# Block products of a decoder layer: high and low weights in two runs, all of the up projection in the 512-column form, and the conv's taps by ScalarE and adding DMAs

## The chip, the cores and the metric

The kernel runs on one core of one Trainium2 chip. The metric is the time of one execution on the device in microseconds (us); lower is better. Before the change it is 2632.48 us, the median of 3 runs (2631.31 to 2634.93).

## What is computed

The reference is one decoder layer over 512 tokens of width 2048, in float32. Cut to what matters here:

```python
proj = x @ w_in                        # (512, 2048) @ (2048, 12288)
u, gate_b, gate_c, q, k, v = split(proj)
y_conv = gate_b * causal_conv3(gate_c * u, conv_w)
y_attn = dilated_window_attention(q, k, v)      # three patterns, merged
x = layernorm(ALPHA * x + concat(y_conv, y_attn) @ w_out)
up = causal_conv3(x @ w_up, ffn_conv_w) + ffn_conv_b   # (512, 2048) @ (2048, 11264)
a, g = split(up)
out = layernorm(ALPHA * x + (silu(g) * a) @ w_down)

def causal_conv3(x, w):                # along the tokens, zero before the first
    return w[0] * x[t-2] + w[1] * x[t-1] + w[2] * x[t]
```

The change touches the two projections `x @ w_in` and `x @ w_up`, and the conv behind the second.

## The kernel before

**High and low parts.** A float32 matrix is kept as two matrices in the format float32r, which TensorE multiplies: a rounded copy `hi` and the rest `lo = x - hi`. A product of two matrices is hi·hi + hi·lo + lo·hi. ScalarE makes `hi` of a weight block (L217), VectorE makes `lo` (L220); both are 128x1024, and both are made up to four blocks ahead of TensorE (the ring `RING = 4`, tiles `whi` and `wlo`).

**Pairs and products.** The projections are cut into pairs of two 128-column strips of the weights: 48 pairs for `w_in`, 44 for `w_up` (`FT`). A pair is computed by Winograd's form of Strassen's scheme: the weights of a pair are four blocks B11, B12, B21, B22, the activations four blocks A11 to A22, and seven products (numbered 1 to 7 in the table `PROD`) replace eight. Four of them take sums of weight blocks, T1 to T4, which VectorE makes with one 128x1024 subtraction each (L207), into tiles `tt` of their own. The products of a pair gather in four PSUM regions: x1 takes products 1, 6, 7; x2 takes 2; x3 takes 5, 3; x4 takes 4. ScalarE copies a region out ("snapshot") after product 1 (x1), 5 (x3) and 6 (x1), before the next product of that region adds to it. VectorE then adds regions and snapshots together (`combine`) into the pair's output tile `o`.

**Two forms of a product.** In the narrow form (`product`, L362 to L374) each of 8 weight slices takes three matmuls with 256 columns: hi·hi (L371), hi·lo (L372), lo·hi (L373), 24 in all. In the 512-column form (`product_wide`, L342 to L352) hi·hi and hi·lo are one matmul with 512 columns (L349), followed by one with 256 (L351), 16 in all; region x2 or another then fills a whole PSUM bank, its halves are still to be added, and `combine` (L418) has four parts with two VectorE instructions each (L427 and L1129 or L683/L687) where the narrow form has two with one each (L667). The part of x4 also takes a ScalarE copy of x1 (L424).

**Which pair takes which form.** Pair 0 of each projection is computed in plain products; of pairs 1 to 5 ("pre-pairs") products 1 and 2 are computed early, while the activations' sums are still being made, and the other five in the narrow form. In the input projection all 42 other pairs take the 512-column form. In the up projection `every=3` (L456, L1131) gives it to the 13 pairs from 6 on whose number divides by 3; the other 25 take the narrow form.

**What sets the order.** Nothing is scheduled by a planner: each engine runs its instructions as they are written. For each product the program writes the matmuls, the snapshot, then `free` (L254), which lets the next weight block be read (`front`, L202: T sum and `hi`) and the one before it be finished (`back`, L219: `lo`), and then `tick` (L321), which runs work that `later(n, ...)` put off by n products. A `combine` is put off by 2. The order of a pair's products is the list `MAIN = [1, 5, 6, 3, 7, 4, 2]` (`LAST` for the last pair); pre-pairs take it without 1 and 2. Weights come in by SP's queue into `RAWS = 3` tiles `raw` of 1 MB, and a tile is loaded again when all blocks in it have been used.

**Behind a pair of the up projection** (`done3`, L1107): ScalarE scales both strips by the conv's tap 2 and adds the bias (L1112); one product later VectorE adds taps 1 and 0 of the gate strip (`taps`, L691 to L694, two instructions) and ScalarE takes Silu (L1116); two products later VectorE adds the taps of the value strip, and three products later it multiplies both (L1119); a DMA from POOL's queue writes the result to DRAM (L1120). POOL's queue holds nothing else in this stage.

## Time and profile before

| | |
|---|---|
| median of 3 runs | 2632.48 us |
| profiled execution, its own time | 2634.48 us |
| its span, first to last instruction | 2632.7 us |
| granted TensorE clock, mean | 0.997 |
| TensorE (PE) busy | 2595.9 us, 99% |
| weight loads (PEld) busy | 2323.1 us, 88% |
| VectorE (DVE) busy | 2157.0 us, 82% |
| ScalarE (ACT) busy | 1211.6 us, 46% |
| GpSimd (POOL) busy | 125.7 us, 5% |

How to read it: the profile is one execution, 1.8 us of whose time lies outside the span. PE counts as busy while a matmul is in its pipeline, so neighbouring matmuls overlap in it, and the sum of a group's durations is more than what the group takes: for the pace one reads the starts in the timeline. In the timeline a row has start, duration, engine, line, operation, output<-inputs, shapes, count, and in brackets the idle time of the engine before it with what ended it. The input projection runs to about 974 us, the attention, the output projection and the first layer norm to about 1245 us, the up projection to 2140 us, the down projection to the end.

### The profile page before, as it was taken

What the parts mean: (1) busy time and instruction counts of PE and PEld (TensorE: products, weight loads), DVE (VectorE), ACT (ScalarE), POOL (GpSimd) and SP (SyncE); (2) the same over time, 40 slices, a digit from 0 to 9 for tenths busy, and PEclk for the clock granted to TensorE, in tenths of its full rate; (3) what the DMA queues carried; (4) which work ended last, traced back from release to release, by engine and by line L of the source; (5) the groups of instructions that cost most, each with busy time, mean ns of one, the idle gap of its engine ahead of it and who ended that gap; (6) DMA issues with size and microseconds to landing.
All of it is one profiled execution on the core that took longest, in us unless ns stands there. A gap on an engine that the chain in (4) does not pass through costs nothing.

```text
span 2632.7 us, 39148 instructions
## 1 busy us (share of the span) xinstructions
PE 2595.9 (99%) x16034; PEld 2323.1 (88%) x16034; DVE 2157.0 (82%) x2575; ACT 1211.6 (46%) x1617; POOL 125.7 (5%) x217
## 2 busy tenths in 40 slices
PE   9999999999999989999999999999999999999997
PEld 8988888888888878888999999999999988888886
DVE  7989888888888877657899999999998966765557
ACT  5544444444444444434655555555555553222220
POOL 0000100000000002220000000000000000000000
PEclk9999999999999999999999999999999999999999
DMA  7422543333333357653543333333333353434331
GB/s 243 169 102 108 182 148 129 132 138 132 128 140 133 125 208 257 220 184 105 184 148 125 118 119 112 121 122 116 123 118 119 125 204 140 152 124 160 112 128 64
DMA packets 70229, 376.34 MB, mean 143 GB/s; under 512 B 9921, under 2 KB 13793, under 8 KB 35361
## 3 DMA queue, kind: packets, MB, share of 16 engines
q1 hardware_dynamic: 51680, 311.47, 33.6%
q0 software_dynamic: 18368, 62.36, 6.5%
q8 instruction: 126, 2.06, 0.3%
q14 instruction: 55, 0.44, 0.1%
HBM read 328.61 MB, written 48.84 MB: 143 GB/s over the span
## 4 chain that ended last, share of the span: by engine, by line
PE 90%; DVE 5%; DMA 2%; ACT 2%; issue 1%; SPq 0%; POOL 0%; DVEq 0%; ACTq 0%
PE bk L349 27%; PE bk L351 13%; PE bk L514 8%; PE bk L516 8%; PE bk L515 8%; PE bk L371 8%; PE bk L372 8%; PE bk L373 8%; DVE wlo L220 1%; DVE tt L207 1%; DMA raw<-in_w_in_dram 1%; DMA ycr<-yc_d 1%; PE bk L848 1%; ACT whi L217 1%; PE bk L794 0%
## 5 line engine op out<-in xcount | busy, mean ns | idle before, releaser
L217 ACT ACTIVATE whi<-raw 128x1024 fp32r<-128x1024 f32 x394 | 414.5, 1057 | 586.5 <-PE bk L516 210.4
L349 PE MATMUL bk<-S,whi 128*128 128x512 f32 x1760 | 624.4, 399 | 1.4 <-ACT s L446 1.4
L220 DVE TENSOR_TENSOR wlo<-raw,whi 128x1024 fp32r<-128x1024 f32 x394 | 480.0, 1221 | 151.3 <-ACT whi L217 149.8
L217 ACT ACTIVATE whi<-tt 128x1024 fp32r<-128x1024 f32 x360 | 381.2, 1059 | 364.2 <-PE bk L349 157.4
L351 PE MATMUL bk<-S,wlo 128*128 128x256 f32 x1760 | 494.1, 281 | 0.0
L349 PE MATMUL bk<-A,whi 128*128 128x512 f32 x1320 | 469.9, 399 | 0.0
L220 DVE TENSOR_TENSOR wlo<-tt,whi 128x1024 fp32r<-128x1024 f32 x360 | 439.4, 1221 | 33.7 <-ACT whi L217 30.1
L349 PEld LDWEIGHTS bk<-S,whi 128*128 128x128 f32 x1760 | 330.7, 188 | 84.5 <-ACT s L446 2.1
L351 PE MATMUL bk<-A,wlo 128*128 128x256 f32 x1320 | 370.7, 281 | 0.0
L351 PEld LDWEIGHTS bk<-S,wlo 128*128 128x128 f32 x1760 | 332.4, 189 | 0.0
L371 PE MATMUL bk<-S,whi 128*128 128x256 f32 x1152 | 326.5, 283 | 1.8 <-ACT sm L467 0.9
L372 PE MATMUL bk<-S,whi 128*128 128x256 f32 x1152 | 326.0, 283 | 0.0
L373 PE MATMUL bk<-S,wlo 128*128 128x256 f32 x1152 | 326.0, 283 | 0.0
L349 PEld LDWEIGHTS bk<-A,whi 128*128 128x128 f32 x1320 | 248.1, 188 | 62.4 <-issue 1.5
L371 PE MATMUL bk<-A,whi 128*128 128x256 f32 x936 | 265.9, 284 | 2.2 <-ACT A L312 1.2
L373 PE MATMUL bk<-A,wlo 128*128 128x256 f32 x936 | 265.3, 283 | 2.6 <-DVE wlo L220 2.6
L372 PE MATMUL bk<-A,whi 128*128 128x256 f32 x936 | 265.0, 283 | 0.9 <-DVE A L313 0.9
L351 PEld LDWEIGHTS bk<-A,wlo 128*128 128x128 f32 x1320 | 249.4, 189 | 0.0
L371 PEld LDWEIGHTS bk<-S,whi 128*128 128x128 f32 x1152 | 221.1, 192 | 2.8 <-ACT z L467 1.7
L372 PEld LDWEIGHTS bk<-S,whi 128*128 128x128 f32 x1152 | 221.1, 192 | 0.0
L373 PEld LDWEIGHTS bk<-S,wlo 128*128 128x128 f32 x1152 | 221.1, 192 | 0.0
L207 DVE TENSOR_TENSOR tt<-raw,tt 128x1024 f32<-128x1024 f32 x180 | 219.1, 1217 | 0.0
(206 smaller groups left out, 4154.0 us busy)
## 6 DMA issues: line engine op xcount, KB each, us to landing
raw<-in_w_in_dram SPq DMA_DIRECT2D x97, 1024.0 KB, 4.9
raw<-in_w_up_dram SPq DMA_DIRECT2D x89, 1024.0 KB, 5.3
raw<-in_w_down_dram SPq DMA_DIRECT2D x44, 1024.0 KB, 4.9
qkv_d<-o POOLq DMA_DIRECT2D x36, 512.0 KB, 3.8
raw<-in_w_out_dram SPq DMA_DIRECT2D x16, 1024.0 KB, 7.3
act_d<-z POOLq DMA_DIRECT2D x44, 256.0 KB, 5.1
qk<-qkv_d SPq DMA_DIRECT2D x7, 1536.0 KB, 10.3
ar<-act_d SPq DMA_DIRECT2D x9, 1024.0 KB, 7.0
```

What stands on the lines that cost most here:

```text
L207: nc.vector.tensor_sub(self.src, v[0], prev)
L217: nc.scalar.activation(self.hi, self.src, AF.Copy)
L220: nc.vector.tensor_sub(self.lo, self.src, self.hi.bitcast(F32))
L349: mm(ps, op.hi[:, w], X[xn].both(k), start=first and k == 0, stop=False, skip_group_check=True)
L351: mm(ps[:, 256:], op.lo[:, w], X[xn][0][:, k], start=False, stop=last and k == 7, skip_group_check=True)
L371: mm(ps, op.hi[:, w], xh[:, k], start=first and k == 0, stop=False, skip_group_check=True)
L372: mm(ps, op.hi[:, w], xl[:, k], start=False, stop=False, skip_group_check=True)
L373: mm(ps, op.lo[:, w], xh[:, k], start=False, stop=last and k == 7, skip_group_check=True)
L514: mm(banks[n], yh[:, tt], op.hi[:, w], start=first and i == 0, stop=False)
L515: mm(banks[n], yh[:, tt], op.lo[:, w], start=False, stop=False)
L516: mm(banks[n], yl[:, tt], op.hi[:, w], start=False, stop=last and i == 1)
L848: nc.tensor.transpose(ps[:, i * P:(i + 1) * P], src[:, n, s:s + P], ident)
```

## The change

1. **High weights first.** In both forms of a product the 8 slices of `hi` run first, then the 8 slices of `lo`. Before, each slice's `lo` matmul followed its `hi`.
2. **All pairs of the up projection from 6 on take the 512-column form** (`every` goes).
3. **Weight sums in place.** T1 and T2 are written over B12, T3 over B11, T4 over B21, inside the `raw` tile; the `tt` tiles go, and `RAWS` is 4. What T2 overwrites must have been used, so the order of products changes: `MAIN` is `[1, 5, 2, 6, 3, 7, 4]` for all pairs, and the pre-pairs take `REST = [5, 3, 6, 7, 4]`. The sums of activations (`s_first`, `s_rest`) use tiles `o` as scratch.
4. **Conv taps of the up projection by ScalarE and DMAs.** For every pair but the last, `done3` has ScalarE multiply both strips by tap 1 into a tile `t` and by tap 0 in place, and two DMAs from POOL's queue add them, shifted by 1 and 2 tokens, to `cv` (`accum_op=OP.add`). Silu follows 7 products later (`TAPS`), the multiplication 8.
5. Tiles: `o` has 5 buffers in this stage, `z` has 4; `cv` is now a tile `o`.

```diff
-RAWS = 3
+RAWS = 4
+TAPS = 7
-MAIN = [1, 5, 6, 3, 7, 4, 2]
-LAST = [1, 5, 2, 6, 3, 7, 4]
+MAIN = [1, 5, 2, 6, 3, 7, 4]
+REST = [5, 3, 6, 7, 4]
...
             if self.kind[0] == "T":
-                self.src = tt_tile()
-                prev = v[1] if len(v) > 1 else self.box["T1" if self.kind == "T2" else "T2"]
-                nc.vector.tensor_sub(self.src, v[0], prev)
-                self.box[self.kind] = self.src
+                b = self.box
+                if self.kind == "T1":
+                    b["T"] = v[0]
+                    nc.vector.tensor_sub(b["T"], v[0], v[1])
+                elif self.kind == "T2":
+                    nc.vector.tensor_sub(b["T"], v[0], b["T"])
+                else:
+                    nc.vector.tensor_sub(v[0], v[0], b["T"])
+                self.src = b["T"] if self.kind in ("T1", "T2") else v[0]
...
-        parts = {"B11": [b11], "B21": [b21], "B22": [b22], "T1": [b12, b11], "T2": [b22], "T3": [b12, b22],
-                 "T4": [b21]}
+        parts = {"B11": [b11], "B21": [b21], "B22": [b22], "T1": [b12, b11], "T2": [b22, b12], "T3": [b11, b12],
+                 "T4": [b21, b12]}
...
-            mm(ps, op.hi[:, w], X[xn].both(k), start=first and k == 0, stop=False,
-               skip_group_check=True)
+            mm(ps, op.hi[:, w], X[xn].both(k), start=first and k == 0, stop=False, skip_group_check=True)
+        for k in range(8):
+            w = slice(k * P, (k + 1) * P)
             mm(ps[:, 256:], op.lo[:, w], X[xn][0][:, k], start=False, stop=last and k == 7, skip_group_check=True)
...
     def done3(j, o):
         o = o.rearrange("p (f h) t -> p f (h t)", f=2)
-        cv = [stile3() for _ in range(2)]
+        cv = otile3().rearrange("p (f h) t -> p f (h t)", f=2)
         for f in range(2):
             ft = j + f * FT
-            nc.scalar.activation(cv[f], o[:, f], AF.Identity, bias=fw_t[:, ft, 3:4], scale=fw_t[:, ft, 2:3])
+            nc.scalar.activation(cv[:, f], o[:, f], AF.Identity, bias=fw_t[:, ft, 3:4], scale=fw_t[:, ft, 2:3])
+        if j < FT - 1:
+            for sh in (1, 2):
+                t = otile3().rearrange("p (f h) t -> p f (h t)", f=2) if sh == 1 else o
+                for f in range(2):
+                    ft = j + f * FT
+                    nc.scalar.activation(t[:, f], o[:, f], AF.Copy, scale=fw_t[:, ft, 2 - sh:3 - sh])
+                nc.gpsimd.dma_start(cv[:, :, sh:], t[:, :, :S - sh], accum_op=OP.add)
...
-        later(1, gate)
-        later(2, lambda: taps(cv[0], o[:, 0], fw_t[:, j]))
-        later(3, mul)
+        later(1 if j == FT - 1 else TAPS, gate)
+        later(2 if j == FT - 1 else TAPS + 1, mul)
...
-    run_pairs(plan3, X, stile3, otile3, bands, done3, act_first, block3, 3)
+    run_pairs(plan3, X, stile3, otile3, bands, done3, act_first, block3)
```

Three places in the order of the instructions. First, on PE, product 6 of a pair in the input projection (S are the chunks of the activation sum S2, `whi` and `wlo` the weight block's two parts, `bk` the PSUM bank), the first six of eight slices of it before (of each two slices that read alike, one):

```order
L349 MATMUL bk_203_1608<-S_66_440,whi_1574 128x512
L351 MATMUL bk_203_1608<-S_66_440,wlo_1575 128x256
...
L349 MATMUL bk_203_1608<-S_76_514,whi_1574 128x512
L351 MATMUL bk_203_1608<-S_76_514,wlo_1575 128x256
...
L349 MATMUL bk_203_1608<-S_85_585,whi_1574 128x512
L351 MATMUL bk_203_1608<-S_85_585,wlo_1575 128x256
```

and the whole of such a product now:

```order
L353 MATMUL bk_206_1756<-S_67_442,whi_1750 128x512 x2
L353 MATMUL bk_206_1756<-S_77_516,whi_1750 128x512 x2
L353 MATMUL bk_206_1756<-S_86_587,whi_1750 128x512 x2
L353 MATMUL bk_206_1756<-S_93_662,whi_1750 128x512 x2
L356 MATMUL bk_206_1756<-S_67_442,wlo_1751 128x256 x2
L356 MATMUL bk_206_1756<-S_77_516,wlo_1751 128x256 x2
L356 MATMUL bk_206_1756<-S_86_587,wlo_1751 128x256 x2
L356 MATMUL bk_206_1756<-S_93_662,wlo_1751 128x256 x2
```

The alternation of 512 and 256 columns has become a run of eight of each, and `wlo` is first read eight matmuls later.

Second, on ACT, the stretch behind a finished pair of the up projection in the 512-column form. Before (L446 are the snapshots of products 1, 5 and 6 into `z`, L217 makes `whi`, L1112 is the conv's tap 2, L1116 is Silu):

```order
L217 ACTIVATE whi_18000<-raw_17847 128x1024
L446 ACTIVATE z_18023<-bk_2680_18006 128x512
L217 ACTIVATE whi_18027<-tt_18025 128x1024
L1112 ACTIVATE z_18032<-o_18004,fw_t 128x512
L1112 ACTIVATE z_18033<-o_18004,fw_t 128x512
L446 ACTIVATE z_18053<-bk_2687_18036 128x512
L217 ACTIVATE whi_18057<-tt_18055 128x1024
L1116 ACTIVATE z_18033<-z_18033 128x512
L446 ACTIVATE z_18082<-bk_2680_18006 128x512
L217 ACTIVATE whi_18084<-raw_17847 128x1024
```

and now (L453 are the snapshots, L221 makes `whi`, L1133 is Silu of the pair before, L431 the copy of x1, L1121 tap 2 into `cv`, L1127 taps 1 and 0):

```order
L221 ACTIVATE whi_15736<-raw_15486 128x1024
L453 ACTIVATE z_15759<-bk_2247_15742 128x512
L221 ACTIVATE whi_15761<-raw_15488 128x1024
L1133 ACTIVATE o_15588<-o_15588 128x512
L431 ACTIVATE z_15766<-bk_2220_15560 128x512
L1121 ACTIVATE o_15770<-o_15672,fw_t 128x512 x2
L1127 ACTIVATE o_15773<-o_15672,fw_t 128x512 x2
L1127 ACTIVATE o_15672<-o_15672,fw_t 128x512 x2
L453 ACTIVATE z_15797<-bk_2254_15780 128x512
L221 ACTIVATE whi_15800<-raw_15486 128x1024
L221 ACTIVATE whi_15824<-raw_15488 128x1024
L453 ACTIVATE z_15844<-bk_2247_15742 128x512
```

Between the snapshot of product 1 and that of product 5 stood three instructions (a weight block and two tap copies); now there are nine.

Third, on ACT, the second pre-pair of the input projection. Before (`sm` takes the snapshots of products 1 and 5, `sn` those of 6 and 7; the blocks `whi` are those of the end of this pair and the start of the next; L705 belongs to the mixer's conv):

```order
L467 ACTIVATE sm_946<-bk_34_182 128x256
L467 ACTIVATE sm_946<-bk_126_949 128x256
L217 ACTIVATE whi_977<-tt_975 128x1024
L705 ACTIVATE o_817<-o_944,cw_t 128x512 x2
L467 ACTIVATE sn_947<-bk_34_182 128x256
L217 ACTIVATE whi_1014<-tt_1012 128x1024
L217 ACTIVATE whi_1048<-tt_1046 128x1024
L467 ACTIVATE sn_947<-bk_34_182 128x256
L217 ACTIVATE whi_1079<-raw_981 128x1024
```

and now:

```order
L474 ACTIVATE sm_941<-bk_35_184 128x256
L474 ACTIVATE sm_941<-bk_120_944 128x256
L221 ACTIVATE whi_971<-raw_654 128x1024
L711 ACTIVATE o_813<-o_939,cw_t 128x512 x2
L221 ACTIVATE whi_1004<-raw_847 128x1024
L474 ACTIVATE sn_942<-bk_35_184 128x256
L221 ACTIVATE whi_1039<-raw_849 128x1024
L474 ACTIVATE sn_942<-bk_35_184 128x256
L221 ACTIVATE whi_1071<-raw_847 128x1024
```

The snapshot of product 6 (the first `sn`) stands one product later, and that of product 7 follows it after one block instead of two: product 7, which adds to the same region, now follows product 6 at once, and product 3 follows product 5, with whose region it shares x3.

More of the change, by code (lines that the diff above doesn't have):

```diff
@@ L183, in load_next @@
         st["load"] += 1
-    def tt_tile():
-        return wpool.tile([P, UNIT], F32, tag="tt", name=nm("tt"), bufs=3)
     class Op:
@@ L290, in plan @@
         for p in range(nplain, n):
-            seqs.append((p, [q for q in (LAST if p == n - 1 else MAIN) if p >= nplain + npre or q > 2], False))
+            seqs.append((p, MAIN if p >= nplain + npre else REST, False))
         return seqs
@@ L372, in product @@
                 mm(ps, op.hi[:, w], xl[:, k], start=False, stop=False, skip_group_check=True)
+            for k in range(8):
+                w = slice(k * P, (k + 1) * P)
                 mm(ps, op.lo[:, w], xh[:, k], start=False, stop=last and k == 7, skip_group_check=True)
@@ L454, in run_wide, with run_pairs @@
                 hook(p, q)
-    def run_pairs(pl, X, stile, otile, bands, done, hook=None, put_block=None, every=1):
+    def run_pairs(pl, X, stile, otile, bands, done, hook=None, put_block=None):
         for p, seq, pre in pl:
@@ L459, in run_pairs @@
                 continue
-            if 1 in seq and put_block and p % every == 0:
+            if 1 in seq and put_block:
                 run_wide(p, seq, X, stile, otile, put_block, done, hook)
@@ L579, in layer_kernel, with otile1 @@
     tp = mkpool(tps, "tp1", "right")
+    def otile1():
+        return tp.tile([P, 4, 256], F32, tag="o", name=nm("o"), bufs=3)
     def x_load(i, k):
@@ L586, in x_split @@
         split(X[n][0][:, k:k + 2], X[n][1][:, k:k + 2], raw["S2"][k // 2][:, i])
-    wt = tt_tile()[:, :256 + P]
+    wt = otile1().rearrange("p a t -> p (a t)")[:, :256 + P]
     nc.vector.memset(wt, 0.0)
@@ L621, in layer_kernel @@
         plan_work(XS + i // 2, x_split, 1, 2 * i)
-        plan_work(XF[i], s_first, X, raw, 2 * i)
-        plan_work(XR[i], s_rest, X, raw, 2 * i)
+        plan_work(XF[i], s_first, X, raw, 2 * i, otile1)
+        plan_work(XR[i], s_rest, X, raw, 2 * i, otile1)
     hook = schedule(todo)
@@ L636, in layer_kernel @@
     nc.sync.dma_start(gb_t, lnc)
-    def otile1():
-        return tp.tile([P, 4, 256], F32, tag="o", name=nm("o"), bufs=3)
     def bias_setup(g=0):
@@ L945, in otile3 @@
     def otile3():
-        return chp.tile([P, 4, 256], F32, tag="o", name=nm("o"), bufs=2)
+        return chp.tile([P, 4, 256], F32, tag="o", name=nm("o"), bufs=5)
     def keep3():
@@ L951, in stile3, with ztiles @@
     def stile3(b=None):
-        return zbp.tile([P, 512], F32, tag="z", name=nm("z"), bufs=8)
-    def ztile(t):
-        return stile3() if t >= 2 else zap.tile([P, 512], F32, tag="z", name=nm("z"), bufs=8)
-    z = [[ztile(t) for c in range(4)] for t in range(4)]
+        return zbp.tile([P, 512], F32, tag="z", name=nm("z"), bufs=4)
+    def ztiles(t):
+        if t == 2:
+            return [o.rearrange("p (a b) t -> p a (b t)", a=2)[:, i] for o in (otile3(), otile3()) for i in range(2)]
+        return [stile3() if t == 3 else zap.tile([P, 512], F32, tag="z", name=nm("z"), bufs=8) for c in range(4)]
+    z = [ztiles(t) for t in range(4)]
     for c in range(4):
@@ L1073, in layer_kernel @@
         plan_work(HF + 2 * i + 1, tr_k, 2 * i + 1, 1, raw["S4"])
-        plan_work(HF + 2 * i + 1, s_first, X, raw, 2 * i)
-        plan_work(HR[i], s_rest, X, raw, 2 * i)
+        plan_work(HF + 2 * i + 1, s_first, X, raw, 2 * i, otile3)
+        plan_work(HR[i], s_rest, X, raw, 2 * i, otile3)
     hook = schedule(todo)
```

20 lines of the change are left out of this document (11 added, 9 removed).

## The prediction

> **What bounds the kernel now.** I read the page first, then the busy time by stretches, then PE's timeline in each stage, since the pace of the matmuls is all that can change the time of a stage in which PE never waits.
>
> ```profile
> span 2632.7 us, 39148 instructions
> PE 2595.9 (99%) x16034; PEld 2323.1 (88%) x16034; DVE 2157.0 (82%) x2575; ACT 1211.6 (46%) x1617; POOL 125.7 (5%) x217
> PE 90%; DVE 5%; DMA 2%; ACT 2%; issue 1%; SPq 0%; POOL 0%; DVEq 0%; ACTq 0%
> ```
>
> PE is busy for 99% of the span and carries 90% of the chain that ended last (third row). So the kernel is bound by TensorE, and an edit pays where it shortens TensorE's own work. How near the others are shows in two stretches of 200 and 100 us, one in each projection (PE, PEld, DVE, ACT, POOL busy, clock, DMA share, GB/s):
>
> ```profile
> 400.00:600.00 200.00, 200.00 (x1135) 173.42 (x1134) 174.88 (x192) 96.77 (x112) 7.16 (x10) 1.00 0.37 132
> 1700.00:1800.00 100.00, 100.00 (x782) 97.32 (x781) 91.46 (x100) 53.57 (x72) 2.71 (x5) 1.00 0.35 119
> ```
>
> VectorE stands at 87% in the input projection and at 91% in the up projection. The paces come from the starts of matmuls in PE's timeline: the 512-column form, then the narrow form, then, from the down projection, 512-column matmuls that follow one another.
>
> ```profile
> 599.61 0.40 PE L349 MATMUL bk<-A,whi 128*128 128x512 f32 x1
> ...
> 627.88 0.40 PE L349 MATMUL bk<-S,whi 128*128 128x512 f32 x1
> ```
>
> ```profile
> 1470.05 0.28 PE L371 MATMUL bk<-S,whi 128*128 128x256 f32 x1
> ...
> 1475.81 0.28 PE L371 MATMUL bk<-A,whi 128*128 128x256 f32 x1
> ```
>
> ```profile
> 2249.72 0.39 PE L514 MATMUL bk<-whi,ah 128*128 128x512 f32 x1
> ...
> 2255.84 0.39 PE L514 MATMUL bk<-whi,ah 128*128 128x512 f32 x1
> ```
>
> Between the first two rows lie 80 slices (ten products): 28.27 us, 0.353 for a 512 and a 256, 2.827 a product. Between the second two lie 48 matmuls (two products): 5.76 us, 0.120 each, 2.88 a product. Between the last two lie 27: 6.12 us, 0.227 each. So the two forms differ by only 0.05 us a product, and a 512 and a 256, each among its like, would take 0.227 + 0.120 = 0.347 where the alternation takes 0.353.
>
> ```profile
> L349 PE MATMUL bk<-A,whi x312: 395/398/403, 1379.0 to 2119.7; 128*128 128x512 f32 x156
> L371 PE MATMUL bk<-A,whi x603: 281/283/283, 1377.9 to 2139.9; 128*128 128x256 f32 x151
> ```
>
> Pairs 6 to 43 of the up projection run from 1379.0 to about 2140 (both rows, with the last slices): 761 us, 20.03 a pair. The 13 wide pairs (91 products at 2.827) and 25 narrow (175 at 2.88) make 257 + 504 = 761: PE does not wait there at all.
>
> **The change, part by part.**
>
> *High weights first.* A product becomes eight 512s and eight 256s: 8 x 0.347, plus about 0.01 for the two changes of width, 2.78 us against 2.827. The input projection has 42 such pairs, 294 products: 294 x 0.047 = **-13.8 us**. VectorE's 87% becomes 89% of the shorter time. [...]
>
> *All pairs wide.* Pairs 6 to 43 now take 266 x 2.78 = 739.5 us if PE still never waits: **-21.8 us**. What covers that is VectorE and ScalarE.
>
> ```profile
> 1701.02 0.69 DVE L427 TENSOR_TENSOR z<-bk,z 128x512 f32<-128x512 f32 x1 [1.61 <-ACT z L424]
> 1701.75 0.43 DVE L1129 TENSOR_TENSOR o<-z 128x256 f32<-128x256 f32 x1
> 1702.09 1.22 DVE L207 TENSOR_TENSOR tt<-raw,raw 128x1024 f32<-128x1024 f32 x1
> 1703.23 1.22 DVE L220 TENSOR_TENSOR wlo<-raw,whi 128x1024 fp32r<-128x1024 f32 x1
> L693 DVE SCALAR_TENSOR_TENSOR z<-o,fw_t,z 128x510 f32<-128x510 f32 x88 | 66.0, 750 | 3.1
> L1119 DVE TENSOR_TENSOR z<-z,z 128x512 f32<-128x512 f32 x44 | 30.1, 684 | 0.1
> ```
>
> From start to start VectorE pays 0.73 for a region's addition, 0.34 for the half's, 1.14 for a 128x1024 subtraction. A pair has 7 `lo`, 4 sums, 4 + 4 additions and the multiplication (684 ns, less the overlap, 0.6): 11 x 1.14 + 4 x 1.07 + 0.6 = 17.4 us of 19.5. Without the taps it fits; with them (four of 750 ns, less the overlap, 2.7 us) it would not, which is why taps move. The sums in place cost VectorE the same; they hold a `raw` tile until its pair's last block, and a fourth tile pays for that.
>
> *Taps on ScalarE.* This is the step that I expect to cost.
>
> ```profile
> 1682.56 0.60 ACT L446 ACTIVATE z<-bk 128x512 f32<-128x512 f32 x1 [1.84 <-PE bk L351]
> 1683.05 1.05 ACT L217 ACTIVATE whi<-tt 128x1024 fp32r<-128x1024 f32 x1
> 1684.00 1.51 ACT L1112 ACTIVATE z<-o,fw_t 128x512 f32<-128x512 f32 x2
> 1685.41 0.58 ACT L446 ACTIVATE z<-bk 128x512 f32<-128x512 f32 x1
> 1687.18 0.63 ACT L1116 ACTIVATE z<-z 128x512 f32<-128x512 f32 x1 [0.23 <-DVE z L693]
> 1700.41 0.58 ACT L424 ACTIVATE z<-bk 128x512 f32<-128x512 f32 x1
> 1702.39 0.38 ACT L467 ACTIVATE z<-bk 128x256 f32<-128x256 f32 x1 [1.40 <-PE bk L373]
> L705 ACT ACTIVATE o<-o,cw_t x8: 709/716/727, 86.2 to 247.2; 128x512 f32<-128x512 f32 x8
> ```
>
> ```profile
> 1702.19 0.28 PE L371 MATMUL bk<-S,whi 128*128 128x256 f32 x1
> PE bk L349 <- ACT s L446: 1.4, 2, 0.7
> PE bk L371 <- ACT sm L467: 0.9, 1, 0.9
> ```
>
> Take the end of a pair's product 1 as zero. A snapshot starts 0.20 after the next product (1702.19 to 1702.39); the next instruction starts 0.49 later (1682.56 to 1683.05), the one after a block 0.95 later, after Silu about 0.54 (length less 0.09, as in the other rows). So in the order now: snapshot 0.20, block 0.69, Silu 1.64, copy of x1 2.18, VectorE's addition 2.79 (0.61 after the copy, as at 1700.41 and 1701.02), its half 3.52, done 3.95; two tap-2 copies to 5.4 (1.41 for two); two tap-1 copies at 0.63 each (716 ns, less the overlap) to 6.65; two tap-0 copies in place, which wait for the read before them, to 8.0; snapshot of product 5 done at 8.6, TensorE free to go on at about 8.7. Product 3 adds to that region and could start at 3 x 2.78 = 8.34. So TensorE waits **0.4 us in each of 38 pairs, +15 us**. The bounds: nothing, if these copies run together more tightly; 0.95 us (+36), if each costs what L1112 does (0.71) and the in-place ones wait in full. That TensorE does stop for a late snapshot shows in the last two rows: 0.7 and 0.9 us at the longest. VectorE's 17.4 us, and some 1.7 of waiting for the block that is late behind the copies, bring it to the next pair's addition at 2.79 + 19.1 = 21.9, before that pair's copy is there (19.9 + 2.79), so its queue does not decide.
>
> *Pre-pairs.* In `REST` product 3 follows 5, and 7 follows 6, which share a region, and the snapshot lies between: 0.20 + 0.38 + about 0.05 = 0.63 us of waiting, twice in each of 10 pre-pairs, **+12 us**. In the five of the up projection the tap copies stand ahead of the second snapshot (more), while VectorE's taps go, which hold that stage back now (less); bounds 6 and 22.
>
> *Adding DMAs.* Each waits for the copies; the second also for the landing of the first; Silu of a pair, a pair later, for both. The multiplied result's DMA stands behind the next pair's two on POOL's queue; the tile that it frees is wanted three pairs later.
>
> ```profile
> raw<-in_w_up_dram SPq DMA_DIRECT2D x89, 1024.0 KB, 5.3
> qkv_d<-o POOLq DMA_DIRECT2D x36, 512.0 KB, 3.8
> act_d<-z POOLq DMA_DIRECT2D x44, 256.0 KB, 5.1
> ```
>
> No row shows an adding DMA. The nearest are 512 KB from POOL's queue in 3.8 us, and 256 KB in this stage in 5.1; an adding one also reads what it adds to. I take 5 to 6 us, which is hidden: the first goes out at about 6.9, the second lands by 19, and Silu comes at 19.9 + 1.64 = 21.5. Each may take (21.5 - 6.9 - 0.4)/2 = 7.1 us before it costs. By the Trainium skill ("DMA: Bandwidth & Descriptors", "Anatomy of one DMA") a DMA from this queue takes 2.0 us and 436 KB per us, 3.2 us here; it gives no price for the adding.
>
> *The fourth raw tile and the later `lo`.*
>
> ```profile
> 1256.98 5.25 DMA raw<-in_w_up_dram
> 1246.26 1.23 DVE wlo L220
> ```
>
> At the start of the up projection the chain waits for a block that could only be loaded once a tile was free (first row), and on `lo` blocks such as the second. A fourth tile starts that load earlier, and PE wants `lo` 1.8 us (8 x 0.227) later: **-5 us** there and at the kernel's start, between 0 and -9.
>
> *The hand-over* to the down projection: the first loads of `act_d` now stand on POOL's queue behind the last pairs' adding DMAs, some 7 us later: +3 us, between 0 and 6.
>
> *Sum:* -13.8 - 21.8 + 15 + 12 - 5 + 3 = -10.6 us. From the profiled execution's own time, 2634.5 (1.8 above its span), that is 2623.9; against the median of 2632.5, **2622**.
>
> **The rivals.**
>
> *The order is worth nothing* (the alternation's extra has another cause, and runs of eight take 0.353 too). Then the input projection stays, the wide pairs take 7 x 2.827 + 0.25 = 20.04 against 20.03, and pre-pairs, start and hand-over leave +10: 2643, slower. Against it: 0.227 and 0.120 are both measured in this run. [...]
>
> *The adding DMAs become the clock of the pair*, the one that ends on the other side for sure. From Silu on, a pair's loop is Silu, copy, addition, four copies (5.1 us), 0.4 to issue, and two landings one after the other; with landings of 8 us it takes 21.5 to 21.7 us instead of 19.9. ScalarE then stands still before Silu and with it blocks and snapshots: 38 x 1.8 = +68, 2690. It decides from 7.1 us on. For it: raw loads of 1 MB run beside them at 5.3 us. Against it: 3.8 us for as many bytes.
>
> *ScalarE is never late*, and the snapshot waits vanish among copies that overlap better: without the 15 us, 2607.
>
> **How the numbers follow.** The forecast (2612 to 2634) has 0.42, order worth nothing 0.14, slow adding DMAs 0.18, no waiting on ScalarE 0.26. The range reaches from 2592 (the last case with its start gain in full) to 2660 (the first of the slow landings, and the forecast with the dearest copies, 2643): left out are about 0.05 below and 0.13 above. A measurement of this kernel can tell about 0.2%, 5.3 us, from no change. Faster by more is 0.30 of the forecast's 0.42, all of the last case and a hundredth of the others: 0.57. Within are 0.11 of the forecast, 0.03 and 0.01 of the first two rivals: 0.15. Slower has the rest, 0.28.
>
> **What would show it.** In the profile after: L353 rows 0.227 apart and L356 rows 0.120, a product of the input projection in 2.78; PE waits for the snapshot (L453) of some 0.4 us a pair in the up projection and for L474 about 20 times 0.6; the adding DMAs landing in 5 to 6 us, Silu (L1133) without a wait for them. I am wrong if L1133 waits for a DMA, if products take 2.83, or if VectorE's additions come later than ScalarE's copies.

## The result, and the profile after

The changed kernel takes **2678.59 us** (median of 4 runs, 2673.5 to 2682.59), beside 2632.84 us (2631.31 to 2634.93) for the kernel before: a ratio of 1.0172, 95% interval 1.0153 to 1.0191. It is slower by 46 us, where the forecast was 2622 us and its range ended at 2660. First the page of the kernel after (span, busy time, and the chain that ended last by engine and by line):

```profile
span 2680.2 us, 36599 instructions
PE 2592.3 (97%) x14634; PEld 2264.6 (84%) x14634; DVE 2108.9 (79%) x2553; ACT 1322.3 (49%) x1789; POOL 229.1 (9%) x303
PE 62%; DMA 22%; ACT 6%; issue 5%; DVE 4%; POOL 0%; SPq 0%; POOLq 0%; DVEq 0%; ACTq 0%
PE bk L353 20%; DMA o<-o 20%; PE bk L356 10%; PE bk L523 8%; PE bk L522 8%; PE bk L521 8%; ACT o L1127 2%; PE bk L376 2%; PE bk L380 2%; PE bk L377 2%; ACT o L1121 1%; DVE z L434 1%; ACT o L1133 1%; DVE wlo L224 1%; ACT z L431 1%
```

PE is still busy for 97% of the span, but it carries only 62% of the chain, where it carried 90%. A fifth of the span now hangs on one group, the adding DMAs `o<-o`. Their rows in the page's last part, KB each and median us from issue to landing:

```profile
raw<-in_w_up_dram SPq DMA_DIRECT2D x89, 1024.0 KB, 7.8
o<-o POOLq DMA_DIRECT2D x43, 511.0 KB, 5.0
o<-o POOLq DMA_DIRECT2D x43, 510.0 KB, 9.6
...
act_d<-o POOLq DMA_DIRECT2D x44, 256.0 KB, 9.5
```

The first of a pair lands after 5.0 us, the second after 9.6. The raw loads went from 5.3 to 7.8, the write of the gated product from 5.1 to 9.5.

Where the 47.5 us between the two spans arise is read from the starts of matmuls, first in the input projection (first and last start at the end of each row), after and before:

```profile
L353 PE MATMUL bk<-S,whi x1344: 387/393/500, 148.9 to 966.2; 128*128 128x512 f32 x192
```

```profile
L349 PE MATMUL bk<-S,whi x1344: 392/398/505, 142.0 to 971.0; 128*128 128x512 f32 x192
```

These rows span 817.3 and 829.0 us; 0.85 of the difference is only the last high slice's earlier place in its product. So the 294 products cost 10.9 us less, 0.037 each (2.793 for 2.830). They start 6.9 us later. The pairs 6 to 43 of the up projection, the first and the last kind of matmul in them after the change, then the last kind before it:

```profile
L353 PE MATMUL bk<-A,whi x912: 389/391/398, 1375.0 to 2170.6; 128*128 128x512 f32 x183
```

```profile
L356 PE MATMUL bk<-A,wlo x912: 277/283/283, 1376.8 to 2171.7; 128*128 128x256 f32 x183
```

```profile
L373 PE MATMUL bk<-A,wlo x604: 280/283/283, 1377.8 to 2140.1; 128*128 128x256 f32 x151
```

From the first start to the last that is 796.7 us, 20.96 a pair, where it was 761.1 (1379.0 to 2140.1). What the two engines waited for between 1400 and 2150 us (us in total, times, longest), ScalarE first, then TensorE:

```profile
ACT o L1133 <- DMA o<-o: 37.0, 33, 1.9
```

```profile
PE bk L353 <- ACT z L453: 38.7, 33, 2.0
```

Silu (L1133) waits for an adding DMA in nearly every pair, which the forecast gave as the sign that it is wrong, and TensorE waits 1.2 us for the snapshot of product 5 behind it. In three pairs these waits are the longest, 1.8 to 2.0 us, and each time the granted clock then stands at half for 3.4 us. The first of the three (PE, PEld, DVE, ACT, POOL busy, clock, DMA share, GB/s):

```profile
1450.60:1454.00 3.40, 3.40 (x12) 2.81 (x12) 3.19 (x4) 2.52 (x4) 0.00 (x0) 0.50 1.04 180
```

These three pairs take 23.2 to 23.4 us and the ones behind them 19.7 to 19.8; together the six take some 4 us more than six others.

The stages add up so: 6.9 late into the input projection's pairs, -10.9 in them, -3.6 from there to the up projection, +3.6 in its early pairs, **+35.6** in its pairs 6 to 43, and **+15.9** from there to the end; together 47.5.

The chain of the kernel after, for one pair in the middle (start, length, what; pieces called issue and pieces under 0.1 us are left out):

```profile
1694.97 0.63 ACT o L1133
1695.60 0.49 ACT z L431
1696.12 0.70 DVE z L434
1696.84 0.44 DVE o L1147
1698.03 0.81 ACT o L1121
1698.83 1.24 ACT o L1127 x2
1700.35 5.79 DMA o<-o
1706.77 9.42 DMA o<-o
1716.27 0.63 ACT o L1133
```

This is a closed loop. Silu of pair p-1 is written ahead of the copy of x1 of pair p on ScalarE; that copy lets VectorE finish pair p, then come the bias copies, two tap copies, the first landing, the second landing, and the next Silu. From Silu to Silu it is 21.30 us, of which 15.21 are the landings; TensorE's seven products would take 19.55. No matmul is on it, so TensorE follows it.

Why the second landing is the longer one shows in the share of the 16 DMA engines that each queue holds (q1 is SP's, with the weight loads, q0 is POOL's), from its issue at 1706.77 to 1711.5, and then from 1711.5 to its landing at 1716.2 (packets, MB, share):

```profile
q1 hardware_dynamic: 218, 1.56, 92.4%
q0 software_dynamic: 25, 0.05, 5.9%
...
q0 software_dynamic: 325, 0.73, 69.0%
q1 hardware_dynamic: 15, 0.08, 4.2%
```

In the first half the engines work on the two raw loads that SP has issued 2.8 and 1.6 us earlier, and the adding DMA moves next to nothing; its own transfer fills the second half, which is about as long as the whole landing of the first one. It is so in all 38 pairs: in the first half of that landing SP's queue holds 89% or more of the engines' time. The second adding DMA is hardly slower as a transfer; it lands late because it stands behind two loads.

At the end of the up projection the chain reads:

```profile
2168.78 11.87 DMA ar<-act_d
2180.67 1.07 ACT A L316
...
2184.04 1.23 DVE wlo L224
2185.31 0.80 PE bk L522
2186.11 0.43 PE bk L523
...
2191.23 0.30 PE bk L523
2191.76 0.23 PE bk L522
```

The first operand of the down projection is requested at 2168.78, 2.9 us ahead of the up projection's last matmul, and lands 11.9 us later. TensorE's first matmul there starts at 2181.8. What TensorE waits for from 2160 to 2200 us:

```profile
PE bk L521 <- ACT A L316: 9.8, 1, 9.8
PE bk L522 <- DVE wlo L224: 2.7, 1, 2.7
```

It waits 9.8 us for ScalarE's part of the operand, then 2.7 us for a low part. Then, to 2191, a 512-column matmul takes 0.43 us instead of 0.23: the granted clock is 0.50 from 2174.2 to 2191.2. By the Trainium skill ("TensorE: Matmul & The Clock Gate", section "What's actually happening") the array's clock is halved after an idle window of about 3.4 us and comes back after a busy one. The halved pace agrees with it; the clock fell 2.2 us into the first wait and came back 6 us after the second. The three drops in the pairs do not fit it: there TensorE had been idle for only 1.8 to 2.0 us.

### The profile page after: what moved, and what is told of

Same layout as the page of the kernel before. It is cut to its first block, busy times and chain, and to the rows that moved or that the text cites. A ratio compares the mean times of both kernels' runs of the same rounds, so it can differ in the third digit from the quotient of the medians.

```text
span 2680.2 us, 36599 instructions
## 1 busy us (share of the span) xinstructions
PE 2592.3 (97%) x14634; PEld 2264.6 (84%) x14634; DVE 2108.9 (79%) x2553; ACT 1322.3 (49%) x1789; POOL 229.1 (9%) x303
## 3 DMA queue, kind: packets, MB, share of 16 engines
q0 software_dynamic: 41760, 107.32, 16.1%
## 4 chain that ended last, share of the span: by engine, by line
PE 62%; DMA 22%; ACT 6%; issue 5%; DVE 4%; POOL 0%; SPq 0%; POOLq 0%; DVEq 0%; ACTq 0%
PE bk L353 20%; DMA o<-o 20%; PE bk L356 10%; PE bk L523 8%; PE bk L522 8%; PE bk L521 8%; ACT o L1127 2%; PE bk L376 2%; PE bk L380 2%; PE bk L377 2%; ACT o L1121 1%; DVE z L434 1%; ACT o L1133 1%; DVE wlo L224 1%; ACT z L431 1%
## 5 line engine op out<-in xcount | busy, mean ns | idle before, releaser
L221 ACT ACTIVATE whi<-raw 128x1024 fp32r<-128x1024 f32 x754 | 787.6, 1056 | 868.3 <-PE bk L523 212.6
L224 DVE TENSOR_TENSOR wlo<-raw,whi 128x1024 fp32r<-128x1024 f32 x754 | 916.6, 1221 | 229.1 <-ACT whi L221 220.8
L353 PEld LDWEIGHTS bk<-S,whi 128*128 128x128 f32 x2560 | 461.5, 189 | 130.0 <-ACT z L453 46.3
L356 PEld LDWEIGHTS bk<-S,wlo 128*128 128x128 f32 x2560 | 351.3, 191 | 25.5
L356 PE MATMUL bk<-S,wlo 128*128 128x256 f32 x2560 | 358.4, 283 | 0.0
L356 PE MATMUL bk<-A,wlo 128*128 128x256 f32 x1920 | 267.7, 282 | 0.0
L521 PE MATMUL bk<-whi,A 128*128 128x512 f32 x480 | 188.1, 392 | 9.8 <-ACT A L316 9.8
L522 PE MATMUL bk<-wlo,A 128*128 128x512 f32 x480 | 188.1, 392 | 2.7 <-DVE wlo L224 2.7
L523 PE MATMUL bk<-whi,A 128*128 128x512 f32 x480 | 187.8, 391 | 0.0
L453 ACT ACTIVATE s<-bk 128x512 f32<-128x512 f32 x126 | 75.2, 597 | 129.9 <-PE bk L356 129.9
L1127 ACT ACTIVATE o<-o,fw_t 128x512 f32<-128x512 f32 x172 | 109.6, 709 | 1.6 <-DMA o<-o 1.6
L209 DVE TENSOR_TENSOR raw<-raw,raw 128x1024 f32<-128x1024 f32 x90 | 109.7, 1219 | 0.3
L211 DVE TENSOR_TENSOR raw<-raw,raw 128x1024 f32<-128x1024 f32 x90 | 109.8, 1220 | 0.0
L211 DVE TENSOR_TENSOR raw<-raw 128x1024 f32<-128x1024 f32 x90 | 109.7, 1219 | 0.0
```

What stands on the lines that cost most here:

```text
L209: nc.vector.tensor_sub(b["T"], v[0], b["T"])
L211: nc.vector.tensor_sub(v[0], v[0], b["T"])
L221: nc.scalar.activation(self.hi, self.src, AF.Copy)
L224: nc.vector.tensor_sub(self.lo, self.src, self.hi.bitcast(F32))
L353: mm(ps, op.hi[:, w], X[xn].both(k), start=first and k == 0, stop=False, skip_group_check=True)
L356: mm(ps[:, 256:], op.lo[:, w], X[xn][0][:, k], start=False, stop=last and k == 7, skip_group_check=True)
```

## The experiments

Four theories. **A**: the landings of the adding DMAs close the loop above. **B**: the burst of copies on ScalarE ahead of product 5's snapshot makes TensorE wait, whatever the DMAs do (my forecast's own term). **C**: the adds slow the other transfers. And for the end of the stage: the loads stand behind the adds on POOL's queue. Each run's ratio is to the kernel before.

**Without the adding DMAs** (the copies stay, and this kernel leaves out two of the three conv taps of these pairs):

```diff
-                nc.gpsimd.dma_start(cv[:, :, sh:], t[:, :, :S - sh], accum_op=OP.add)
```

> The kernel after without the two adding DMAs of each pair (43 pairs); the ScalarE copies that fed them stay, so in these pairs two of the three conv taps are missing from the output. Theory A (the landing of the adding DMAs closes a loop: Silu of pair p-1, copy of x1, sums, bias copies of pair p, tap copies, first landing 5.0 to 5.8 us, second 8.8 to 9.7 us, next Silu, about 21.3 us): the wait of the Silu line for a DMA (37.7 us in the kernel after) is gone, TensorE's wait for the snapshot of product 5 falls from 39.4 us to under 15, pairs 6 to 43 take 19.6 to 20.1 us instead of 20.96 (-33 to -52 us), and the wait of 9.8 us at the hand-over shrinks too since the loads of the down projection's operand stand behind no adding DMA (-8 to -14 us): 2615 to 2640 us. Theory B (the burst of copies on ScalarE ahead of that snapshot is what TensorE waits for, whatever the DMAs do): pairs stay at 20.5 us or more, only the hand-over is repaired: 2648 to 2670 us.

Measured: 2619.97 us, ratio 0.9955 (0.994 to 0.9969). Pairs take 19.77 us, no wait for a snapshot is listed, and TensorE's wait for the down projection's operand is gone: from the last matmul of pair 43 to the end of the span it takes 493.2 us, 492.6 before the change and 508.5 after it. So it is the DMAs that cost, and not the burst: the burst of copies is all there, and pairs take only 0.22 us more than the 19.55 of the products, where the kernel after takes 1.4 more.

**Silu one product later**, all DMAs and copies kept:

```diff
-TAPS = 7
+TAPS = 8
```

> The kernel after with the Silu and the gating multiply of a pair each one product later (8 and 9 instead of 7 and 8): the Silu of pair p-1 then stands behind the copies of pair p on ScalarE and behind its snapshot of product 5, so a late adding DMA no longer holds these up; all DMAs and copies stay. Theory A (loop closed by the landing): the loop is open, TensorE's wait for the snapshot falls to under 15 us, pairs 19.6 to 20.1 us: -33 to -52 us, hand-over as it is: 2627 to 2648 us. Theory B (the ScalarE burst by itself): only the 0.63 us of the Silu itself and its wait leave the stretch ahead of the snapshot, but the eight copies stay: 2660 to 2680 us. Theory C (the adding DMAs are slow by themselves and hold up the raw loads and the writes that share their queues): the wait only moves to VectorE's first sum of the next pair, which needs the buffer that the gated product is written from: 2665 to 2685 us.

Measured: 2628.46 us, 0.9989 (0.998 to 0.9998). One number takes 50 us off. The pairs (first start and last start), then TensorE between 1372 and 2112 us, the busy time by stretches (us, then PE, PEld, DVE, ACT, POOL busy, clock, DMA share, GB/s), then the landings in the same kernel:

```profile
L353 PE MATMUL bk<-A,whi x912: 389/391/398, 1371.2 to 2116.0; 128*128 128x512 f32 x183
L356 PE MATMUL bk<-A,wlo x912: 277/283/283, 1373.1 to 2117.0; 128*128 128x256 f32 x183
```

```profile
1372.00:2112.00 740.00, 740.00 (x4224) 650.61 (x4223) 651.11 (x749) 501.67 (x680) 111.05 (x113) 1.00 0.68 173
```

```profile
o<-o POOLq DMA_DIRECT2D x43, 511.0 KB, 5.0
o<-o POOLq DMA_DIRECT2D x43, 510.0 KB, 9.7
```

PE is never idle, pairs take 19.63 (1371.2 to 2117.0 for 38), and yet the adds land no sooner than they did. Their latency was harmful only because ScalarE's copies for the next pair stood behind the instruction that waited for it. Behind those copies Silu finds its data there. Theory C's wait for the buffer did not come, with every transfer as slow as before. A holds.

**The second tap's copies and DMA one product later**, behind the snapshot:

```diff
-            for sh in (1, 2):
+            def tap(sh):
...
+            tap(1)
+            later(1, lambda: tap(2))
```

> The kernel after with the two ScalarE copies of the second tap, and the issue of its adding DMA, one product later, so behind the snapshot of product 5 (the second DMA waits 5 us for the landing of the first anyway). The burst ahead of the snapshot is two copies (1.4 us) shorter. Theory A (loop closed by the landing): the loop from Silu to Silu holds the same steps or more, so the pair stays at 20.7 us or more: 2668 to 2685 us. Theory B (the burst by itself, of which TensorE waits about 1.1 us a pair): the wait all but goes, -30 to -42 us: 2637 to 2650 us.

Measured: 2672.22 us, 1.0158 (1.0141 to 1.0175); pairs take 20.81 us. ScalarE's wait for the DMA, from 1360 to 2160 us, grew (its line is L1136 here):

```profile
ACT o L1136 <- DMA o<-o: 51.1, 36, 2.4
```

The burst ahead of the snapshot is two copies shorter, and the pair only 0.15 us: ScalarE waits longer at Silu, and TensorE still waits 30.9 us for snapshots, most of it now one product later. B is out as the main cause.

**The order of the weights alone**, in the kernel before (the 512-column form is shown; the narrow form is changed alike):

```diff
             mm(ps, op.hi[:, w], X[xn].both(k), start=first and k == 0, stop=False,
                skip_group_check=True)
+        for k in range(8):
+            w = slice(k * P, (k + 1) * P)
             mm(ps[:, 256:], op.lo[:, w], X[xn][0][:, k], start=False, stop=last and k == 7, skip_group_check=True)
```

> The kernel before with the order of the high and the low weights alone changed (all high products of a weight block, then all low ones), nothing else. If the order is worth what the in-projection of the kernel after showed (2.793 instead of 2.830 us a product): 294 products there are worth -10.9 us, and the 13 wide pairs of the up projection have 91 products, -3.4 us if TensorE sets their time and 0 if VectorE does: 2618 to 2623 us. If the gain of the kernel after in that stretch came from something else that changed with it (four raw tiles, the sums in place of the raw blocks): 2630 to 2634 us.

Measured: 2618.09 us, 0.9947 (0.9933 to 0.9962). Two products in the input projection, one behind the other:

```profile
599.72 2.00 PE L349 MATMUL bk<-S,whi 128*128 128x512 f32 x8
...
602.51 2.00 PE L349 MATMUL bk<-S,whi 128*128 128x512 f32 x8
```

A product takes 2.793 us as in the kernel after, a wide pair 19.55 instead of 19.79, a narrow one of the up projection 20.16 as before. The gain belongs to the order.

**The early pairs' order of before**, on the kernel with the later Silu:

```diff
-REST = [5, 3, 6, 7, 4]
+REST = [5, 6, 3, 7, 4]
```

> The kernel of the run with the Silu one product later (2628.46 us), with the remaining products of the five early pairs in the order of before again (5, 6, 3, 7, 4 in place of 5, 3, 6, 7, 4), in both projections. Theory A (products 5 and 3 and products 6 and 7 write the same half bank one behind the other, and the second waits 0.63 us, and the next weight 0.09 us, for the snapshot of the first): the 3.51 us products of this stretch (nine in the in-projection, ten or so in the up projection) fall to 2.88, 20 waits of 0.72 us less, -11 to -15 us: 2613 to 2618 us. Theory B (the waits come from the weight sums in place of the raw blocks, whatever the order): they move to other products, 2624 to 2632 us.

Measured: 2620.09 us, 0.9952 (0.9936 to 0.9969). (In this run and in the one with three parts mended, T2 is written over T1 before the low part of T1 has been taken, so these kernels leave that low part out in the early pairs.) The input projection's pairs start at 139.4 us instead of 145.0, and its nine products of 3.51 us are 2.88. In the up projection's early pairs there is no gain: products of 3.51 went, others of 3.7 to 5.5 came. So of the 20 waits only about half, those of the input projection, cost time.

**The two loads on SP's queue**, also on the kernel with the later Silu:

```diff
-                nc.gpsimd.dma_start(act[i], act_d[:, 4 * i:4 * i + 4, :])
+                nc.sync.dma_start(act[i], act_d[:, 4 * i:4 * i + 4, :])
```

> The kernel of the run with the Silu one product later (2628.46 us), with the two first loads of the down projection's operand issued on SP's queue in place of POOL's. Theory A (on POOL they stand behind the adding DMAs of the last pairs, whose second one waits for the landing of the first; they land late and TensorE waits 9.9 us for ScalarE's copy of them, and the clock is lower for a while after that idle time): -9 to -15 us: 2613 to 2620 us. Theory B (they are late because the DMA engines themselves are taken up by the adds and the down weights, so another queue changes nothing): 2624 to 2632 us.

Measured: 2615.1 us, 0.994 (0.9925 to 0.9955), 12.9 us less by the ratios. The stretch from 2110 to 2130 us, with the loads on POOL's queue and then on SP's:

```profile
2110.00:2130.00 20.00, 8.09 (x45) 6.57 (x43) 6.32 (x8) 6.28 (x8) 2.88 (x4) 0.81 0.86 264
```

```profile
2110.00:2130.00 20.00, 20.00 (x112) 17.36 (x111) 17.83 (x20) 16.83 (x22) 2.95 (x3) 1.00 0.93 283
```

PE, idle for 12 of 20 us at a granted clock of 0.81, now never stops. On POOL's queue the loads went out 3.0 us before the last pair's last matmul, on SP's 13.8 us before it, and they landed in 5.8 us instead of 13.0. By the Trainium skill ("DMA: Bandwidth & Descriptors", section "Issuing engines are not separate DMA queues") another issuing engine saves only the time to issue. Here it saved more: the wait for the instructions ahead in POOL's queue. In the profiles the stretch from the last matmul of the pairs to the end is 492.7 us again, as before the change.

**All three mended** (the later Silu, the early pairs' order and the loads on SP's queue):

> The kernel after with all three: the Silu one product later, the order of before in the early pairs, the two loads on SP's queue. If the three parts are separate costs as theory A has it (about -50, -13 and -12 us), the sum is 2600 to 2607 us, 26 to 32 us under the kernel before, about 11 to 18 us under the kernel before with the weight order alone (2618.09 us). If the loads or the early pairs were only shifting waits: 2612 to 2628 us.

Measured: 2606.27 us, 0.9905 (0.989 to 0.9919). The parts add up: 1.83% from the later Silu, 0.49% from the queue and 0.37% from the early pairs' order are 2.69%, the whole is 2.67%.

**All pairs wide with the taps on VectorE**, no adding DMAs:

```diff
-        if j < FT - 1:
+        if False:
             for sh in (1, 2):
...
-        later(1 if j == FT - 1 else TAPS, gate)
-        later(2 if j == FT - 1 else TAPS + 1, mul)
+        later(1, gate)
+        later(2, lambda: taps(cv[:, 0], o[:, 0], fw_t[:, j]))
+        later(3, mul)
```

> The kernel after with the conv taps of all pairs on VectorE as before (Silu, second half and gate one, two and three products after the bias copies), no adding DMAs, all pairs still in the wide form. VectorE's work for a pair is then what it has in the kernel after (seven low parts at 1.221, four sums of weights at 1.218, four of 0.686, four of 0.425, one multiply of 0.684: 18.5 us) and four taps at 0.749: 21.5 us, more than TensorE's 19.55. Theory A: VectorE becomes the pair's clock, pairs 21.5 to 22.1 us in place of 20.96, +20 to +43 us, less the hand-over's 10 to 15 us: 2684 to 2712 us. Theory B (wide pairs leave VectorE slack, and the adding DMAs were not needed for them): pairs 19.6 to 20.3 us: 2615 to 2640 us.

Measured: 2640.58 us, 1.004 (1.0025 to 1.0055): some 35 us faster than the kernel after, by the ratios, where I expected it to be slower. VectorE is the clock of the pairs, busy for 98% of the stretch below, but at 20.37 us, not 21.5:

```profile
1376.00:2130.00 754.00, 735.47 (x4161) 641.00 (x4161) 741.46 (x886) 410.16 (x519) 20.00 (x37) 1.00 0.33 117
```

```profile
1706.34 1.53 DVE L699 SCALAR_TENSOR_TENSOR o<-o,fw_t,o 128x511 f32<-128x511 f32 x2
1707.79 1.22 DVE L211 TENSOR_TENSOR raw<-raw,raw 128x1024 f32<-128x1024 f32 x1
1708.93 1.22 DVE L224 TENSOR_TENSOR wlo<-raw,whi 128x1024 fp32r<-128x1024 f32 x1
```

I had summed lengths. From start to start two taps take 1.45 us, and a 128x1024 subtraction 1.14, not 1.22: an instruction on VectorE starts some 80 ns before the one ahead has ended. With the prediction's starts, 17.4 + 2.9 = 20.3, the number was to be had.

**The first sum's low part taken ahead of the second sum**, added to the three mended parts, so that the order of before and the sums in place go together:

```diff
+            if op.kind == "T2":
+                back_upto(i)
             op.front()
```

> The run with the three mended parts (2606.27 us), in which the order of before in the early pairs let the second weight sum overwrite the first one ahead of its low part; here the low part of the first sum is taken ahead of the second sum, so nothing is left out. Theory A: this adds a wait of VectorE for ScalarE's high part once in each of ten early pairs, off TensorE's path in the in-projection, and up to a microsecond each in the up projection: 2604 to 2612 us, 0.8 to 1.0% under the kernel before. Theory B (the order of the early pairs and sums in place do not go together without a wait of the 0.72 us kind): 2612 to 2618 us, no better than the loads on SP's queue without the order (2615.1 us).

Measured: 2647.35 us, 1.0059 (1.0046 to 1.0071): both theories missed, by some 30 us and more. Pairs 6 to 43 take 20.65 us. The edit also hit the wide pairs, where it put the low part of B21 ahead of the second sum. ScalarE's wait for that sum from 1390 to 2090 us, in the kernel with the later Silu and here:

```profile
ACT whi L221 <- DVE raw L209: 94.3, 36, 2.6
```

```profile
ACT whi L221 <- DVE raw L209: 127.9, 34, 4.0
```

It is 1.1 us longer each time, one VectorE subtraction, and what follows on ScalarE, the snapshot of product 5 among it, is late by as much: TensorE waits 24.0 us there for the snapshot, 0 in the other.

**Three raw tiles in that kernel:**

```diff
-RAWS = 4
+RAWS = 3
```

> The kernel of the run beside it with everything mended, with three raw weight tiles in place of four. Theory A (TensorE waits for no raw load in the pairs, the fourth tile was worth nothing like the 5 us of the forecast): 2604 to 2614 us, within 2 us of the run beside it. Theory B (with the adding DMAs a raw load takes 7.3 us instead of 5.3, and with sums in place a raw tile is held up to the last sum of its pair, so three tiles are too few): pairs 20 us or more, 2620 us or more.

Measured: 2653.44 us, 1.0081 (1.0065 to 1.0096), 5.8 us more than the run before by the ratios, with intervals that just overlap. Pairs stay at 20.65. It is at the start of the up projection that the chain waits for a raw load again, as it did before the change:

```profile
1247.27 5.56 DMA raw<-in_w_up_dram
```

**Plain copies in place of the adds**, on the kernel with the later Silu (the last tap's copy then replaces the sum, so the conv of these pairs is not computed):

```diff
-                nc.gpsimd.dma_start(cv[:, :, sh:], t[:, :, :S - sh], accum_op=OP.add)
+                nc.gpsimd.dma_start(cv[:, :, sh:], t[:, :, :S - sh])
```

> The kernel of the run with the Silu one product later (2628.46 us), with both adding DMAs of a pair as plain copies of the same size, source, target, queue and order (the conv of these pairs is then wrong: the last tap's copy replaces the sum). Theory A (the second add lands after 9.7 us because adding is slow in itself or what it is beside slows it as it would a copy): this separates them. If adding is what costs, the landings fall from 5.0 and 9.7 us to about 3 and 5 us and the raw loads from 7.3 towards the 6.4 us of the run without adds. If sharing with the raw loads and the write of the gated product costs, they stay near 5 and 9 us. The time: 2615 to 2630 us in either case, since TensorE sets the pair here.

Measured: 2626.01 us (one run). The landings and the share of the POOL queue's packets (packets, MB, share of the 16 engines):

```profile
q0 software_dynamic: 28000, 107.32, 10.9%
...
o<-o POOLq DMA_DIRECT2D x43, 511.0 KB, 3.1
o<-o POOLq DMA_DIRECT2D x43, 510.0 KB, 8.1
```

The adding itself costs 1.6 to 1.9 us of a landing and takes the queue's packets from 28000 to 41760 and its share from 10.9 to 16.3%. The second landing stays long as a plain copy too, 5 us longer than the first. So that difference is not due to the adding; the shares of the queues above show the raw loads ahead of it.

**Everything mended, the low part ahead in the early pairs alone:**

```diff
+            if op.kind == "T2" and ops[i - 1].kind == "T1":
+                back_upto(i)
             op.front()
```

> As the run with everything mended (2647.35 us), but the low part is taken ahead of the second weight sum only where the block before it is the first sum, which is so in the early pairs alone; the wide pairs keep the order low part behind the sum. Theory A (in that run the pair of VectorE instructions, low part of B21 and second sum, stood the other way round in all wide pairs too; VectorE waited there for ScalarE's high part, which made the second sum and all behind it late, 1.02 us a pair, 20.65 in place of 19.63, 39 us over the pairs): pairs are 19.63 again, 2604 to 2610 us. Theory B (the early pairs' wait is what costs there): 2640 us or more.

Measured: 2608.61 us, 0.9913 (0.9896 to 0.993). Pairs take 19.64 us. This version computes everything and beats both kernels: 22 us under the kernel before and 70 us under the change as it was made. Of the 22, 14 are the weights' order.

## Why the prediction was wrong

The step that failed is the one on the adding DMAs: "I take 5 to 6 us, which is hidden", with "Each may take (21.5 - 6.9 - 0.4)/2 = 7.1 us before it costs". The second landing took 9.6 us, and it lay in a loop of ScalarE's own order, so it set the time of the pair.

- **Adding DMAs**, forecast 0, measured **about +50 us** (what the later Silu gave back; net of what the change gains there, the pairs are 35.6 longer). The first landing was priced rightly, the second not: it was taken from transfers of another stage (512 KB in 3.8 us), while it stands behind two raw loads, and took 9.6. A hint of that was quoted, 256 KB in 5.1 us in this very stage. And the margin was thin: two landings of 7.1 us are 14.2 in all; measured were 14.6 by the medians and 15.2 in the loop shown. The formula for the loop was too short as well: 5.5 us beside the landings, where the chain has 6.1, with 0.6 from the first landing to the second issue; 6.1 and the median landings give 20.7 of the 20.96 measured. The rival named this mechanism, its place and its point of decision, and got 0.18.
- **High weights first**: forecast -13.8, measured -10.9 in the input projection. That the order alone gains is right; a 512 behind a 512 takes 0.231 us here, not the down projection's 0.227. The Trainium skill ("TensorE: Matmul & The Clock Gate", section "Back-to-back issue gap") gives the gap of an isolated matmul by its columns alone, and says that in a stream of weight loads and matmuls both set the spacing. By columns alone the order would be worth nothing; here it took a product from 2.830 to 2.793 us.
- **All pairs wide**, -21.8: in the kernel with the later Silu the pairs take 745.8 us, 15.3 less than before. The missing 6.5 are 3.5 for products of 2.793 instead of 2.78 us, and 0.08 us a pair.
- **Taps on ScalarE**, 0.4 us a pair, +15: with the Silu ahead of the copies, but no DMA to wait for, it is 0.22 (+8); with the Silu behind them, 0.08. The estimate was about twice too large.
- **Early pairs**, +12: the 0.63 us is exact (3.51 for 2.88), but in the up projection other waits stand under it; going back to the old order gave 7 to 10 us by the ratios.
- **Fourth raw tile and later low parts**, -5: the size fits; three tiles cost 5.8 us in the one kernel where they were tried, whose pairs take 20.65. The later low parts were not tried by themselves.
- **Hand-over**, +3, at most 6: measured +15.9, of which the other queue gives back 12.9 by the ratios, and nearly all by the profiles. The loads go out 2.9 us before the last matmul of the pairs, where they went out 13.6 us before it (the row below, against 2140.1): 11 us later, not 7. And idle TensorE lost clock on top: 9.8 + 2.7 us of waiting, then 6 us at half pace, which is some 3 more.

```profile
2126.52 1.07 POOL L1100 DMA_DIRECT2D ar<-act_d  x2 [13.33 <-issue]
```

Two edits that take away no work and no transfer, Silu one product later and the loads on SP's queue, remove both large waits and give 2615.1 us, ratio 0.994. That is no more than the weights' order gives by itself (0.9947): the wide pairs and the moved taps then just pay for the waits that are left. Only with the early pairs mended too does the whole change come out ahead of its first part, by 9 us. Still open is why the DMA engines work off both raw loads before they take up the second adding DMA: no run moved these loads away from it.

## What to carry to other kernels

Before a latency is called hidden, follow the in-order queues: ask what is written behind the instruction that waits for it, and whether that leads back to the transfer's own start. If it does, the latency is part of a period, and no slack elsewhere hides it; writing the waiting instruction behind the producers of the next round opened the loop here at no cost. And price a transfer by what stands on the DMA engines when it is issued, not by its size alone.

## What the runs showed of the hardware

- A DMA of 512 KB from SBUF to SBUF that adds took 5.0 us, as a plain copy 3.1. Issued beside 1 MB loads of SP's queue it took 9.7 and 8.1; in the first half of one such landing of an adding DMA, SP's queue held 92.4% of the 16 engines' time and POOL's 5.9%.
- A 512-column matmul behind another took 0.231 us in the projections and 0.227 in the down projection; a 256 behind a 256 took 0.120.
- After TensorE had been idle for some 12 us, a 512-column matmul took 0.43 us instead of 0.23 for 6 us. In the pairs of the kernel after, waits of 1.78, 1.85 and 2.0 us were each followed by 3.4 us at a granted clock of 0.50; no shorter wait there was.
- On VectorE instructions overlap: a sum of lengths gave 21.5 us where the engine, busy for 98% of the time, took 20.37.
